# Four gate tiles by Strassen's scheme in the values' stage, and the first attention's queries and keys split on 128 partitions

## The chip, the cores and the metric

The kernel runs on one NeuronCore of a Trainium2 chip. The metric is the device time of one execution in microseconds. The core's engines run side by side, each through its own list of instructions in order: TensorE (PE in the profile, its weight loads PEld), VectorE (DVE), ScalarE (ACT), GpSimd (POOL) and SyncE (SP). DMA transfers are issued by SP, ACT and POOL, each into its own queue.

## The reference

One layer of a decoder trunk on 1024 positions and 1024 channels, all in float32.

```python
h = rms_norm(x, pre_mix_g)
proj = h @ w_in                     # 8192 columns
qa, ka, va, qb, kb, vb, gates = split(proj, ...)   # 512 512 512 1536 1536 1536 2048
# first attention: 4 heads, each two softmaxes of 64 dimensions, causal
qa, ka = rope(qa), rope(ka)
oa = (softmax(qa1 ka1) - lam * softmax(qa2 ka2)) @ va
ya = (rms_norm(oa) * 0.8) @ w_a_out
# second attention: 3 dilations x 4 heads of 128 dimensions, windows
yb = merge_of_dilations(qb, kb, vb) @ w_b_out
g_a, g_b = split(sigmoid(gates))
x = x + rms_norm((g_a * ya + g_b * yb) @ w_mix_out)
# gated MLP with a causal convolution of 3 taps
u = conv(rms_norm(x) @ w_up)
x = x + rms_norm((gelu(gate) * val) @ w_down)
```

(The factor 0.8 stands for 1 - lam_init, which is 0.8 lam_init being 0.2.)

## The kernel before

Every matrix product works on float32 operands split into two parts of a shorter format, a high one (ACT copies it, `split`, L149) and the rest (DVE subtracts, L146). `mm3` (L155 to L157) multiplies high by high, low by high and high by low: three matmuls for one product of 128 x 128 by 128 x 512.

The program runs in stages.

*The values' stage.* All values (va and vb, 2048 columns) are made in two sides of 1024 columns (`i` 0 and 1). Each side is a product of 2 x 2 blocks, done by Strassen's scheme in Winograd's form: seven products p1 to p7 for eight. Their left operands are blocks and sums of blocks of the transposed input: `b11`, `b21`, `b12`, `b22` lie in `xh`, `xl`, the sums in `t2`, `t3`, `t4`; a part of the first sum takes the place of `b12` until the product p6 of side 1, when `split_x` restores it. A list `steps_v` gives the order of the 56 steps (product, side, block of 128 rows); one step is 4 x 3 matmuls. `fetch_v` loads a step's weights on SP's queue, `ready_v` adds or subtracts weight blocks where a product needs it (`wz`) and splits them, five steps ahead, and `take_v` moves finished banks of PSUM into the quarters `yv`, which `put_v` sends to memory (`v_d`) on POOL's queue. The steps at which the first side's quarters are sent are in `STORE_AT`; other steps carry the norm, the angles, the sines and the tables of the rotation. Products on the right use the banks of the pools `ps_s` and `pt`, those on the left the pool `acc` and one bank of `ps_o`.

*The first attention.* A head's queries and keys come from `proj_t`, 2 halves x 8 blocks x 3 matmuls for each 128 columns. `rotated` applies the rotation with four copies of 32 partitions on ACT and three instructions on DVE. The two softmaxes of a head lie on partitions 0 to 63 (`u`) and 64 to 127 (`v`). `put_q` writes the high part of each into `a0`, `a1` and the low part into `b0`, `b1`, on 64 partitions each, and after the second half four transfers on POOL's queue (L754) copy them to the other 64 partitions. `put_k` writes the high part on one half of the partitions of `k0`, `k1` and the low part on the other. `attend_a` makes the scores of a block of 128 queries (L784, L785), takes minima and exponentials, joins the two softmaxes (L801), and every second block `turned` transposes them (L713) and `pv` multiplies by the values.

*The gates.* `gate(i)` is `proj_t` for one tile of 128 gate columns; `put_gate` scales it by the norm (DVE, L250) and sends it to memory on ACT's queue. The 16 gate tiles serve as filling work: `START_GATES` of them stand ahead of the first head, the letters g of `A_FILLS` are one gate each in the filling of heads 0 to 3 (p is the next head's projection, v and w the values of the second pair of heads, P, x, V belong to the second attention), and `B_GATES` of them run in the last step of the second attention. `interleave` spreads the filling over the steps of a head.

*Behind it* come the second attention, its merge of three dilations through memory, two output branches that read the gates back, the mixing product, and the MLP.

The order on each engine is written by a planner that simulates the program, with priorities from the code; `later` hangs work onto a count of steps.

Of the kernel before, what the change touches and what calls it, by code (L numbers as in the profile page):

```python
# [24 lines left out]
P = 128  # L25
# [21 lines left out]
NH = NF // 2  # L47
AHEAD, T1_AT, LAST = 4, 5, 7
MIX_UNITS = {3: (0,), 4: (1,), 5: (2, 4), 6: (5,), 7: (6, 3, 7)}
START_GATES, A_FILLS, B_GATES = 1, ("gpgg", "gpvgg", "wgpgg", "xgPVgg"), 3  # L50
SLOTS = 18
LEFT_PAD = 48


XT_BUFS, NORM_AT, ANGLES_AT, SINES_AT, TABLES_AT, STORE_AT = 6, 14, 25, 33, 34, {35: 0, 36: 3, 39: 2, 41: 1}

K_FIRST = (4, 0, 5, 1, 6, 2, 7, 3)
RSQRT_MAGIC = float(0x5F3759DF)
# [29 lines left out]
def trunk(ctx: ExitStack, tc: tile.TileContext, a, out):  # L88
# [252 lines left out]
    def f32(v):  # L341
        return v.bitcast(F32)
# [118 lines left out]
    with ExitStack() as st_y:  # L461
# [6 lines left out]
        def turns(pattern, *ps):  # L468

            ks = [iter(range(4)) for _ in ps]  # L470
            return [(ps[c], 1, next(ks[c])) for c in pattern]

        steps_v += [("p1", 1, k) for k in range(4)] + turns((0, 0, 1, 0, 1, 0, 1, 1), "p5", "p6")
        steps_v += turns((0, 0, 1, 1, 1, 1, 0, 0), "p3", "p7") + [("p4", 1, k) for k in range(4)]
        wz = [t[:, k % 2] for t in [wv.tile([P, 2, 512], F32, tag=f"wz{i}", name="wz") for i in range(2)] for k in range(2)]
        ready, got_v = {}, {}
# [10 lines left out]
        def new_y(name, pool=None):  # L487
            return [(pool or yv).tile([P, 512], F32, tag=f"y{name}{m}", name="yv") for m in range(4)]

        def fetch_v(n):  # L490
            p, i, k = steps_v[n]
            which = {"p1": ((0, 0),), "p2": ((0, 1),), "p5": ((1, 0), (1, 1)), "p6": ((0, 0),), "p7": ((0, 0), (1, 0)),
                     "p4": ((1, 1),), "p3": ((0, 1),)}[p]
            got_v[n] = [load_raw(a["w_v"][j * 4 + k][:, (2 * i + c) * 512 : (2 * i + c + 1) * 512], next(tags), parts=1 if n else 2)
                        for c, j in which]

        def ready_v(n, w=512):
            p, _, k = steps_v[n]
# [54 lines left out]
        quarter = {(0, i): new_y(f"a{i}") for i in range(2)}  # L553
        banks = {}

        def step_v(n):
            p, i, k = steps_v[n]
            x = xs_of[p]
            if p in ("p1", "p2", "p5") and k == 0:
                left = p == "p1"  # L560
                banks[left] = ([psum() for _ in range(3)] + [psum(F32, ps_o, "o")] if left else
                               [psum(F32, q, t) for q, t in ((ps_s, "s"), (pt, "pt")) for _ in range(2)])
            use = banks[p in ("p1", "p6", "p7", "p4")]
            wh, wl = ready.pop(n)
            for m in range(4):
                tk = slice(m * P, (m + 1) * P)
                mm3(use[m], x[0][:, k, tk], x[1][:, k, tk], wh, wl, k == 0 and p in ("p1", "p2", "p5"), k == 3, p in ("p6", "p7", "p4", "p3"))
            if k < 3:
                return
            with tc.high_priority(offset=80):  # L570
                for m in range(4):
                    take_v(p, i, m, use[m])
            if p == "p7" and i == 0:
                for m in range(4):
                    tt(quarter[3, 0][m], banks[False][m], quarter[3, 0][m], ALU.add)
# [56 lines left out]
        for n in range(8, len(steps_v)):  # L632
            p, i, k = steps_v[n]
            while fetched < min(n + (8 if n <= TABLES_AT else 10), len(steps_v)):
                fetch_v(fetched)
                fetched += 1
            while made < min(n + 5, len(steps_v)):
                ready_v(made)
                made += 1
            if 0 <= n - NORM_AT < 11:  # L640
                norm_x(n - NORM_AT)
            if n == NORM_AT + 11:
                lambda_scale()
            if n == TABLES_AT + 2:
                scale_tables(*args)
            if n == TABLES_AT + 4:
                tags = more_tags()
            if n == ANGLES_AT:
                pos = [load_raw(a["positions"][sl].partition_broadcast(P), next(tags)) for sl in halves()]
                args = [tb.tile([P, S], F32, tag=n_, name=n_) for n_ in ("sin", "cos")]  # L650
                angles(pos, *args, tb)
            if n in STORE_AT:
                put_v(STORE_AT[n], 0, True)
            if n == SINES_AT:
                make_sines(*args)
            if n == TABLES_AT:
                turn_norms()
            if k == 0 and (p, i) in places_y:
                q, name, pool = places_y[p, i]
                quarter[q, i] = new_y(name, pool)  # L660
            step_v(n)
            if k == 3 and i and p in ("p1", "p7", "p4", "p3"):
                put_v({"p1": 0, "p7": 3, "p4": 2, "p3": 1}[p], 1, p == "p1")
            if (p, i) == ("p5", 1):

                again.append(load_raw(a["xT"][k][:, 512:], next(tags)))
            if (p, i) == ("p6", 1):
                with behind_marks():
                    split_x(k, halves()[1], again[k])
# [15 lines left out]
                dma(v.rearrange("p (r ih) c -> p r ih c", ih=n)[:, :, ih], src[:, i * 4 // n : (i + 1) * 4 // n, ih])  # L685
        return vs

    def split_values(vs, res):

        with behind_marks():  # L690
            for v in vs:
                res.append(v_tiles())
                split(*res[-1], v)

    def rotated(ps, cos, sin, sl, quarter):
        t1 = rt.tile([P, 512], F32, tag="t1", name="t1")
        t2 = rt.tile([P, 512], F32, tag="t2", name="t2")
        for q in range(P // quarter):
            src, dst = slice((q ^ 1) * quarter, ((q ^ 1) + 1) * quarter), slice(q * quarter, (q + 1) * quarter)
            nc.scalar.activation(t1[dst], ps[src], AF.Copy)  # L700
        nc.vector.tensor_tensor(t2, ps, cos[:, sl], op=ALU.mult)  # L701
        nc.vector.tensor_tensor(t1, t1, sin[:, sl], op=ALU.mult)
        nc.vector.tensor_tensor(t2, t2, t1, op=ALU.add)
        return t2

    def v_tiles():
        return [slot(t, (P, 4, 256)) for t in ("vh", "vl")]
# [34 lines left out]
    def proj_a(h, res):  # L742
        a0, a1, b0, b1, k0, k1 = (slot(n) for n in ("a0", "a1", "b0", "b1", "k0", "k1"))
        res += [a0, a1, b0, b1, k0, k1]

        def put_q(half, sl, ps):
            t = rotated(ps, cos_a, sin_a, sl, 32)
            for part, hi in ((u, a0), (v, a1)):
                nc.scalar.activation(hi[part, sl], t[part], AF.Copy)
            for part, hi, lo in ((u, a0, b0), (v, a1, b1)):  # L750
                nc.vector.tensor_tensor(lo[part, sl], t[part], f32(hi[part, sl]), op=ALU.subtract)
            if half:
                for x, from_, to in ((a0, u, v), (a1, v, u), (b0, u, v), (b1, v, u)):
                    side(x[to], x[from_])  # L754

        def put_k(half, sl, ps):
            t = rotated(ps, cos_a, sin_a, sl, 32)
            for part, kk in ((u, k0), (v, k1)):
                nc.scalar.activation(kk[part, sl], t[part], AF.Copy)
            for part, to, kk in ((u, v, k0), (v, u, k1)):  # L760
                nc.vector.tensor_tensor(kk[to, sl], t[part], f32(kk[part, sl]), op=ALU.subtract)

        yield from proj_t(QA + h * P, put_q)
        yield from proj_t(KA + h * P, put_k)
# [104 lines left out]
        later(1, sums)  # L869
        later(3, norm)  # L870

    free_gates = list(range(2 * KC))

    def gates(n):

# [32 lines left out]
    def once(fn):  # L908

        fn()  # L910
        yield 0
# [13 lines left out]
    with st_a:  # L925
        ops = [[] for _ in range(AH)]
        vs = [[] for _ in range(AH // 2)]
        run(gates(START_GATES)[0])
        run(proj_a(0, ops[0]))
        split_values(fetch_values(1, 0), vs[0])  # L930
        of_pair = []
        for h in range(AH):
            out_sb, pair = {}, []
            todo = [functools.partial(attend_a, h, i, ops[h], vs[h // 2], out_sb, pair) for i in (6, 7, 4, 5, 2, 3, 0, 1)]
            kinds = {
                "p": lambda: (proj_a(h + 1, ops[h + 1]), 8),
                "v": lambda: (once(lambda: of_pair.extend(fetch_values(1, 256))), 0),
                "w": lambda: (once(lambda: split_values(of_pair, vs[1])), 0),
                "g": lambda: gates(1),
                "P": lambda: (proj_b(0, 0, ops_b[steps[0]]), 8),  # L940
                "x": lambda: (once(lambda: fetch_b(0, 0)), 0),
                "V": lambda: (once(lambda: split_b(0, 0)), 0),
            }
            if h + 1 == AH:
                tabs_b += load_tabs(0, 64)
            fills = [kinds[c]() for c in A_FILLS[h]]
            if h + 1 < AH:
                interleave(jobs(todo, a_weight), 52, *fills)
            else:
                interleave(itertools.chain(jobs(todo, a_weight), rest_due(12)), 64, *fills)  # L950
# [851 lines left out]
```

## Time and profile before

| what | value |
|---|---|
| median of three runs | 1685.25 us (1685.08 to 1686.24) |
| the profiled execution | 1684.85 us |
| its span | 1683.1 us |
| instructions | 22937 |
| data read from HBM, written to it | 177.54 MB, 47.86 MB |
| loads of weights from w_in | 96 of 256 KB |
| loads of weights for the values | 71 of 256 KB, 2 of 128 KB |
| stores of gates | 32 of 256 KB on ACT's queue |
| copies of a and b by POOL's queue | 16 of 256 KB |

The span runs from the first to the last instruction of the profiled execution; the device time has a little more around it. In rows of the timeline the first number is the start in us from the beginning of the span, the second the duration in us, and then engine, line, operation, out<-in, shape and count. In rows of groups the total in us and the mean in ns follow the count.

### The profile page before, as it was taken

The numbers are of one execution on the slowest core, as the hardware profiler recorded it, in microseconds if no ns is written. First come the engines' busy times: TensorE is split into PE (matmuls) and PEld (weight loads), VectorE is DVE, ScalarE is ACT, GpSimd is POOL, SyncE is SP. The second block draws the span as 40 slices with busy tenths as digits, with TensorE's granted clock in tenths as the row PEclk, the third lists the DMA queues.
The fourth block names the chain that finished last, engine by engine and source line by source line (L and its number), as shares of the span: only waits on it lengthen the run. The fifth ranks groups of instructions, "written<-read, shape, count | busy, mean of one in ns | idle before, by whom it ended". The sixth has DMA issues, their size and how long they took to land. (4 is left out here: it accounts for less than half of the span.)

```text
span 1683.1 us, 22937 instructions
## 1 busy us (share of the span) xinstructions
PE 1668.5 (99%) x7878; PEld 1394.0 (83%) x7878; DVE 1308.4 (78%) x2430; ACT 913.4 (54%) x1707; POOL 170.2 (10%) x267
## 2 busy tenths in 40 slices
PE   9999999999999999999999999999999999999997
PEld 7888888888888888888888888887888888888886
DVE  8795576877777777788766865988888778799978
ACT  7633574655445677667554533565554455255453
POOL 0031000000000000000123400022211121000000
PEclk9999999999999999999999999999999999999999
DMA  8767421315122212343676532267755655296524
GB/s 269 234 221 266 132 83 62 107 57 147 48 70 75 76 57 78 107 135 105 212 264 223 188 113 89 58 159 172 161 133 132 156 137 126 96 348 214 193 88 150
DMA packets 117253, 241.59 MB, mean 144 GB/s; under 512 B 14528, under 2 KB 23680, under 8 KB 117136
## 3 DMA queue, kind: packets, MB, share of 16 engines
q1 hardware_dynamic: 89296, 171.28, 30.6%
q0 software_dynamic: 23088, 60.45, 15.2%
q10 hardware_dynamic: 4752, 8.39, 1.3%
q8 instruction: 62, 1.02, 0.3%
q14 instruction: 55, 0.45, 0.1%
HBM read 177.54 MB, written 47.86 MB: 134 GB/s over the span
## 5 line engine op out<-in xcount | busy, mean ns | idle before, releaser
L157 PE MATMUL acc<-xl,whi 128*128 128x512 f32 x768 | 302.5, 394 | 0.0
L155 PE MATMUL acc<-xh,whi 128*128 128x512 f32 x768 | 302.0, 393 | 0.0
L156 PE MATMUL acc<-xh,wlo 128*128 128x512 f32 x768 | 301.7, 393 | 0.0
L149 ACT ACTIVATE whi<-raw 128x512 fp32r<-128x512 f32 (+1 forms) x249 | 154.1, 627 | 180.6 <-PE acc L157 115.4
L146 DVE TENSOR_TENSOR wlo<-raw,whi 128x512 fp32r<-128x512 f32 (+1 forms) x249 | 172.2, 700 | 32.8 <-ACT whi L149 27.9
L156 PEld LDWEIGHTS acc<-xh,wlo 128*128 128x128 f32 x768 | 144.4, 188 | 27.9
L157 PEld LDWEIGHTS acc<-xl,whi 128*128 128x128 f32 x768 | 144.4, 188 | 27.7
L155 PEld LDWEIGHTS acc<-xh,whi 128*128 128x128 f32 x768 | 144.5, 188 | 27.3
L155 PE MATMUL acc<-mh,whi 128*128 128x512 f32 x384 | 149.7, 390 | 1.7 <-ACT u L1447 1.3
L156 PE MATMUL acc<-mh,wlo 128*128 128x512 f32 x384 | 149.4, 389 | 0.0
L157 PE MATMUL acc<-ml,whi 128*128 128x512 f32 x384 | 149.1, 389 | 0.0
L700 ACT ACTIVATE t<-acc 64x512 f32<-64x512 f32 (+1 forms) x160 | 94.7, 592 | 62.0 <-PE acc L157 60.4
L149 ACT ACTIVATE whi<-s 128x512 fp32r<-128x512 f32 x80 | 49.8, 627 | 90.7 <-PE acc L157 63.5
L1443 DVE TENSOR_TENSOR u<-acc,u 128x512 f32<-128x512 f32 x100 | 68.5, 687 | 29.1 <-PE acc L157 28.9
L701 DVE TENSOR_TENSOR t<-acc,cos 128x512 f32<-128x512 f32 x64 | 44.2, 690 | 55.4 <-ACT t L700 51.9
L155 PEld LDWEIGHTS acc<-mh,whi 128*128 128x128 f32 x384 | 72.1, 188 | 17.7 <-ACT u L1447 2.2
L157 PEld LDWEIGHTS acc<-ml,whi 128*128 128x128 f32 x384 | 72.1, 188 | 14.9
L156 PEld LDWEIGHTS acc<-mh,wlo 128*128 128x128 f32 x384 | 72.1, 188 | 14.9
L1620 PE MATMUL acc<-whi,wlo 128*128 128x512 f32 x216 | 76.1, 390 | 0.0
L1619 PE MATMUL acc<-whi 128*128 128x512 f32 x216 | 74.8, 389 | 0.0
L1621 PE MATMUL acc<-wlo,whi 128*128 128x512 f32 x216 | 71.6, 390 | 0.0
L787 DVE CUSTOM_DVE_ANT_0 s<-s,mask_a 128x512 f32<-128x512 f32 (+3 forms) x96 | 52.5, 555 | 23.2 <-PE s L785 18.5
(402 smaller groups left out, 4015.2 us busy)
## 6 DMA issues: line engine op xcount, KB each, us to landing
raw<-in_w_in SPq DMA_DIRECT2D x96, 256.0 KB, 2.8
raw<-in_w_v SPq DMA_DIRECT2D x71, 256.0 KB, 4.6
raw<-in_w_up SPq DMA_DIRECT2D x68, 256.0 KB, 3.6
raw<-c_d SPq DMA_DIRECT2D x48, 256.0 KB, 3.6
c_d<-c SPq DMA_DIRECT2D x22, 512.0 KB, 4.0
s<-in_w_up POOLq DMA_DIRECT2D x40, 256.0 KB, 4.2
s<-s POOLq DMA_DIRECT2D x40, 256.0 KB, 3.9
raw<-in_w_down SPq DMA_DIRECT2D x37, 256.0 KB, 3.5
```

What stands on the lines that cost most here:

```text
L146: eng.tensor_tensor(lo, src, hi.bitcast(F32), op=ALU.subtract)
L149: copy = nc.scalar.activation(hi, src, AF.Copy)
L155: nc.tensor.matmul(o, sh, mh, start=first, stop=False, skip_group_check=on)
L156: nc.tensor.matmul(o, sl, mh, start=False, stop=False, skip_group_check=on)
L157: nc.tensor.matmul(o, sh, ml, start=False, stop=last, skip_group_check=on)
L700: nc.scalar.activation(t1[dst], ps[src], AF.Copy)
L701: nc.vector.tensor_tensor(t2, ps, cos[:, sl], op=ALU.mult)
L787: nc.vector.tensor_tensor_reduce(out=s_sb[:, c0:c1], in0=ps, in1=mask, scale=-scale, scalar=3.0e38, op0=ALU.add, op1=ALU.min, accum_out=mx ...
L1443: nc.vector.tensor_tensor(to, made(p), x, op=ALU.add)
L1619: nc.tensor.matmul(banks[m], gh[:, tk], wh, start=f == 0, stop=False)
L1620: nc.tensor.matmul(banks[m], gl[:, tk], wh, start=False, stop=False)
L1621: nc.tensor.matmul(banks[m], gh[:, tk], wl, start=False, stop=f == NH - 1)
```

## The change

Four of the 16 gate tiles, `gate_of(x, c)` = 12 to 15, are made in the values' stage as `PAIRS` = 2 pairs, by the same seven products; here the weights are the stationary operand and the input is the moving one. They stand behind the first side and p1 of the second, 14 steps of 4 x 3 matmuls, product by product with the two pairs in turn. Their results are added up in tiles that the quarters leave free, scaled (DVE) and sent on POOL's queue. One gate leaves the filling of each of heads 0, 1 and 2, and one leaves the last step of the second attention. `STORE_AT` moves the stores of the first side.

The rotation's result is split on all 128 partitions at once, into the tiles t1 and t2, and every piece of 64 partitions is placed by a transfer on POOL's queue: 8 for each half of the queries, 4 for each half of the keys. The values of the second pair of heads are split in halves.

```diff
-START_GATES, A_FILLS, B_GATES = 1, ("gpgg", "gpvgg", "wgpgg", "xgPVgg"), 3
+PAIRS, START_GATES, A_FILLS, B_GATES = 2, 1, ("gpg", "gpvg", "wgpg", "xgPVgg"), 2
-..., STORE_AT = ..., {35: 0, 36: 3, 39: 2, 41: 1}
+..., STORE_AT = ..., {32: 0, 37: 3, 42: 2, 46: 1}
...
-        steps_v += [("p1", 1, k) for k in range(4)] + turns((0, 0, 1, 0, 1, 0, 1, 1), "p5", "p6")
+        steps_v += [("p1", 1, k) for k in range(4)]
+        steps_v += [(p, "gate", x) for p in ("p2", "p1", "p5", "p6", "p7", "p4", "p3") for x in range(PAIRS)]
+        steps_v += turns((0, 0, 1, 0, 1, 0, 1, 1), "p5", "p6")
...
+        def gate_of(x, c):
+            return 2 * (KC - PAIRS + x) + c
...
+            if i == "gate":
+                srcs = [w_in[where[GT + gate_of(k, c) * P]][:, j * 512 : (j + 1) * 512] for c, j in which]
+            else:
+                srcs = [a["w_v"][j * 4 + k][:, (2 * i + c) * 512 : (2 * i + c + 1) * 512] for c, j in which]
+            got_v[n] = [load_raw(src, next(tags), parts=1 if n else 2) for src in srcs]
...
+        def take_gate(p, n, use):
+
+            def put(q):
+                sl = halves()[q % 2]
+                y = gate_y[n][q]
+                tt(y, use if p == "p4" else y, rstd_row[:, sl], ALU.mult)
+                nc.gpsimd.dma_start(gt_d[gate_of(n, q // 2)][:, sl], y)
+
+            y = gate_y[n]
+            if p in ("p2", "p6", "p7"):
+                nc.scalar.activation(y[{"p2": 0, "p6": 1, "p7": 3}[p]], use, AF.Copy)
+            if p == "p1":
+                tt(y[0], use, y[0], ALU.add)
+                put(0)
+            if p == "p7":
+                tt(y[3], banks[n, False], y[3], ALU.add)
+                put(3)
+            if p == "p4":
+                put(2)
+            if p == "p3":
+                tt(y[1], use, y[1], ALU.add)
+                put(1)
+
+        def step_gate(p, n, wh, wl):
+
+            left = p in ("p1", "p6", "p7", "p4")
+            if p in ("p1", "p2"):
+                banks[n, left] = psum(F32, pt, "pt") if left else psum(F32, ps_s, "s")
+            x, use = xs_of[p], banks[n, left]
+            for k in range(4):
+                c = slice(k * P, (k + 1) * P)
+                mm3(use, wh[:, c], wl[:, c], x[0][:, k], x[1][:, k], k == 0 and p in ("p1", "p2", "p5"), k == 3, ...)
+            with tc.high_priority(offset=80):
+                take_gate(p, n, use)
...
+            if (p, i, k) == ("p2", "gate", 0):
+                ya, yb = new_y("a0"), new_y("b3", yw)
+                gate_y.update({x: {0: ya[x], 1: ya[2 + x], 3: yb[x], 2: yb[2 + x]} for x in range(PAIRS)})
...
-    def split_values(vs, res):
+    def split_values(vs, res, parts=4):
...
-                split(*res[-1], v)
+                for b in range(0, 4, parts):
+                    split(*(t[:, b : b + parts] for t in (*res[-1], v)))
...
+        def split_rotated(t):
+            t, other = t
+            hi, lo = other.bitcast(F32R), t.bitcast(F32R)
+            nc.scalar.activation(hi, t, AF.Copy)
+            nc.vector.tensor_tensor(lo, t, other, op=ALU.subtract)
+            return hi, lo
+
         def put_q(half, sl, ps):
-            t = rotated(ps, cos_a, sin_a, sl, 32)
-            for part, hi in ((u, a0), (v, a1)):
-                nc.scalar.activation(hi[part, sl], t[part], AF.Copy)
-            for part, hi, lo in ((u, a0, b0), (v, a1, b1)):
-                nc.vector.tensor_tensor(lo[part, sl], t[part], f32(hi[part, sl]), op=ALU.subtract)
-            if half:
-                for x, from_, to in ((a0, u, v), (a1, v, u), (b0, u, v), (b1, v, u)):
-                    side(x[to], x[from_])
+            t = rotated(ps, cos_a, sin_a, sl, 32, True)
+            hi, lo = split_rotated(t)
+            for x, src, part in ((a0, hi, u), (a1, hi, v), (b0, lo, u), (b1, lo, v)):
+                for to in (u, v):
+                    side(x[to, sl], src[part])
 
         def put_k(half, sl, ps):
-            t = rotated(ps, cos_a, sin_a, sl, 32)
-            for part, kk in ((u, k0), (v, k1)):
-                nc.scalar.activation(kk[part, sl], t[part], AF.Copy)
-            for part, to, kk in ((u, v, k0), (v, u, k1)):
-                nc.vector.tensor_tensor(kk[to, sl], t[part], f32(kk[part, sl]), op=ALU.subtract)
+            t = rotated(ps, cos_a, sin_a, sl, 32, True)
+            hi, lo = split_rotated(t)
+            for x, src, part, to in ((k0, hi, u, u), (k0, lo, u, v), (k1, hi, v, v), (k1, lo, v, u)):
+                side(x[to, sl], src[part])
...
-    free_gates = list(range(2 * KC))
+    free_gates = list(range(2 * (KC - PAIRS)))
...
-                "w": lambda: (once(lambda: split_values(of_pair, vs[1])), 0),
+                "w": lambda: (once(lambda: split_values(of_pair, vs[1], 2)), 0),
```

More of the change, by code (lines that the diff above doesn't have):

```diff
@@ L49 @@
 MIX_UNITS = {3: (0,), 4: (1,), 5: (2, 4), 6: (5,), 7: (6, 3, 7)}
-START_GATES, A_FILLS, B_GATES = 1, ("gpgg", "gpvgg", "wgpgg", "xgPVgg"), 3
+PAIRS, START_GATES, A_FILLS, B_GATES = 2, 1, ("gpg", "gpvg", "wgpg", "xgPVgg"), 2
 SLOTS = 18
 LEFT_PAD = 48
-XT_BUFS, NORM_AT, ANGLES_AT, SINES_AT, TABLES_AT, STORE_AT = 6, 14, 25, 33, 34, {35: 0, 36: 3, 39: 2, 41: 1}
+XT_BUFS, NORM_AT, ANGLES_AT, SINES_AT, TABLES_AT, STORE_AT = 6, 14, 25, 33, 34, {32: 0, 37: 3, 42: 2, 46: 1}
 K_FIRST = (4, 0, 5, 1, 6, 2, 7, 3)
@@ L493, in fetch_v @@
                      "p4": ((1, 1),), "p3": ((0, 1),)}[p]
-            got_v[n] = [load_raw(a["w_v"][j * 4 + k][:, (2 * i + c) * 512 : (2 * i + c + 1) * 512], next(tags), parts=1 if n else 2)
-                        for c, j in which]
+            if i == "gate":
[3 more added lines that the diff above has]
+            got_v[n] = [load_raw(src, next(tags), parts=1 if n else 2) for src in srcs]
         def ready_v(n, w=512):
@@ L554, in trunk @@
         banks = {}
+        gate_y = {}
+        def take_gate(p, n, use):
[25 more added lines that the diff above has]
+                c = slice(k * P, (k + 1) * P)
+                mm3(use, wh[:, c], wl[:, c], x[0][:, k], x[1][:, k], k == 0 and p in ("p1", "p2", "p5"), k == 3, p in ("p6", "p7", "p4", "p3"))
+            with tc.high_priority(offset=80):
+                take_gate(p, n, use)
         def step_v(n):
             p, i, k = steps_v[n]
+            if i == "gate":
+                step_gate(p, k, *ready.pop(n))
+                return
             x = xs_of[p]
@@ L692, in split_values, with rotated @@
                 res.append(v_tiles())
-                split(*res[-1], v)
-    def rotated(ps, cos, sin, sl, quarter):
+                for b in range(0, 4, parts):
+                    split(*(t[:, b : b + parts] for t in (*res[-1], v)))
+    def rotated(ps, cos, sin, sl, quarter, both=False):
         t1 = rt.tile([P, 512], F32, tag="t1", name="t1")
@@ L703, in rotated @@
         nc.vector.tensor_tensor(t2, t2, t1, op=ALU.add)
-        return t2
+        return (t2, t1) if both else t2
     def v_tiles():
```

## The prediction

> **What bounds the kernel now.** I read the first part of the page (busy time), then the waits of TensorE, then the matmuls in order of time, and last the busy time of every engine stage by stage.
>
> ```profile
> span 1683.1 us, 22937 instructions
> PE 1668.5 (99%) x7878; PEld 1394.0 (83%) x7878; DVE 1308.4 (78%) x2430; ACT 913.4 (54%) x1707; POOL 170.2 (10%) x267
> ```
>
> The waits of TensorE (who, for whom: us in total, times, longest):
>
> ```profile
> PE acc L155 <- ACT xh L387: 1.4, 1, 1.4
> PE acc L155 <- DVE ya L1211: 1.4, 2, 0.9
> PE acc L155 <- ACT u L1447: 1.3, 1, 1.3
> PE pt L594 <- DVE t4l L591: 1.2, 1, 1.2
> PE acc L155 <- ACT mh L149: 0.3, 1, 0.3
> PE acc L156 <- DVE xl L383: 0.2, 1, 0.2
> ```
>
> The reader is to see that the six waits add up to 5.8 us of 1683. TensorE is fed from end to end, so the time is the sum of its instructions, and a matmul taken away is worth what it occupies, until something starves. What it occupies is not the duration that the page gives. The group of the projections' and gates' matmuls, and three rows from the first projection (start, us, what), then the last row of that unbroken run:
>
> ```profile
> L157 PE MATMUL acc<-xl,whi 128*128 128x512 f32 x768 | 302.5, 394 | 0.0
> ...
> 178.07 0.39 PE L155 MATMUL acc<-xh,whi 128*128 128x512 f32 x1
> 178.30 0.39 PE L156 MATMUL acc<-xh,wlo 128*128 128x512 f32 x1
> 178.53 0.39 PE L157 MATMUL acc<-xl,whi 128*128 128x512 f32 x1
> ...
> 203.46 0.39 PE L156 MATMUL acc<-xh,wlo 128*128 128x512 f32 x1
> ```
>
> Each lasts 0.39 us, but the next one starts 0.23 us later: they overlap. From 178.07 to 203.46 there are 113 matmuls, hence 25.39 / 112 = 0.2267 us each. That is the price I use.
>
> The stages (us; busy time and instructions of PE, PEld, DVE, ACT, POOL; clock, DMA share, GB/s). The values' stage ends at 161.8; then the first gate and head 0's projections; heads 0, 1, 2 of the first attention, each from its first score to the next head's; the end of the second attention, where the last gates are; the first output branch:
>
> ```profile
> 100.00:161.80 61.80, 61.80 (x279) 51.23 (x278) 47.63 (x84) 25.08 (x41) 21.48 (x33) 1.00 0.76 262
> 161.80:203.70 41.90, 41.90 (x187) 34.70 (x186) 19.14 (x29) 20.71 (x34) 4.44 (x9) 1.00 0.54 162
> 203.70:275.50 71.80, 71.80 (x351) 60.31 (x350) 53.96 (x128) 43.48 (x90) 2.06 (x4) 1.00 0.25 78
> 275.50:350.10 74.60, 74.60 (x380) 63.11 (x379) 56.88 (x154) 41.50 (x89) 2.06 (x4) 1.00 0.28 89
> 350.10:426.10 76.00, 76.00 (x387) 64.27 (x386) 59.28 (x156) 44.17 (x92) 2.07 (x4) 1.00 0.38 104
> 815.00:852.50 37.50, 37.50 (x194) 31.86 (x193) 24.07 (x62) 23.63 (x48) 6.44 (x11) 1.00 0.74 252
> 852.50:905.00 52.50, 51.14 (x230) 41.77 (x229) 34.47 (x59) 15.84 (x25) 12.98 (x23) 1.00 0.70 232
> ```
>
> TensorE is busy in all of every stage but the last, where its 1.4 us wait for DVE lies.
>
> **The gates' matmuls.** A gate is 2 halves x 8 blocks x 3 = 48 matmuls, four are 192. By the scheme a pair is 7 products x 4 blocks x 3 = 84, two pairs 168. All are 128x512. So 24 go: 24 x 0.2267 = **5.44 us less**. The values' stage grows by 168 x 0.2267 = 38.1 us; each of heads 0, 1, 2 and the last step of the second attention shrinks by 48 x 0.2267 = 10.88 us.
>
> **What the values' stage takes on.** Rows for its new work, all in DVE's groups of the first 500 us and in the page's DMA issues:
>
> ```profile
> L146 DVE TENSOR_TENSOR wlo<-wz,whi 128x512 fp32r<-128x512 f32 x24 | 16.2, 689 | 0.1
> L345 DVE TENSOR_TENSOR wz<-raw,wz 128x512 f32<-128x512 f32 x8 | 5.5, 692 | 9.6 <-DMA raw<-in_w_v 9.6
> L250 DVE TENSOR_TENSOR gate<-acc,rstd_row 128x512 f32<-128x512 f32 x26 | 17.9, 688 | 10.4 <-PE acc L157 10.4
> raw<-in_w_in SPq DMA_DIRECT2D x96, 256.0 KB, 2.8
> v_d<-yv POOLq DMA_DIRECT2D x32, 256.0 KB, 5.2
> ```
>
> DVE: 14 splits, 8 sums of weights (p5, p6, p7, p3 of each pair) and 14 sums and scalings of results, 36 x 0.69 = 24.8 us in 38.1. The late part of the stage had 47.63 of 61.8 (77%) and gets 72.4 of 99.9 (72%). The 18 weight loads on SP's queue (1, 1, 2, 1, 2, 1, 1 a pair, against 8 before) and 8 stores now on POOL's queue are 6.8 MB in 38.1 us, 179 GB/s, below the 262 of that part. The values' stores that move to later steps leave more room. Operands are made five steps (5 x 12 x 0.2267 = 13.6 us) ahead. So I take 0. One seam is tight: the values' p5 takes over the banks that the gates' last p3 leaves, and DVE reads the last of these (0.69 us) while three matmuls (0.68 us) run. Bounds 0 and one step, 2.7 us; I take 0.3, since TensorE can begin on the other two banks.
>
> **What the heads lose.** A gate takes 2 splits and 2 scalings of DVE with it, 4 x 0.69 = 2.8 us. The new rotation takes one DVE and one ACT instruction from each of four half projections a head: two on 64 partitions become one on 128, and the former cost as much as one on 128:
>
> ```profile
> L761 DVE TENSOR_TENSOR k<-t,k 64x512 fp32r<-64x512 f32 x16 | 11.0, 687 | 0.5
> L749 ACT ACTIVATE a<-t x16: 615/630/633, 183.3 to 381.3; 64x512 fp32r<-64x512 f32 x16
> ```
>
> That is another 2.8 us of DVE and 2.5 of ACT. DVE in heads 0 to 2: (53.96 - 5.6) / 60.9 = 79%, 80%, 82%, from 75, 76 and 78. No engine becomes the bound. The chain can still be too slow: DVE makes the probabilities (L801), TensorE turns them (L713). The closest in-order pair I found is in head 1:
>
> ```profile
> 326.89 1.02 DVE L801 SCALAR_TENSOR_TENSOR s<-s,ratio 128x768 f32<-128x768 f32 x1
> 329.51 0.27 PE L713 MATMUL pt<-ident,s 128*128 128x128 f32 x1
> ```
>
> It has 329.51 - 327.91 = 1.6 us to spare; a pair of query blocks gets 10.88 / 4 = 2.7 us shorter. If the chain kept its pace it would lose 1.1 us here. The two rotations save it 1.3 us of DVE and ACT each. Bounds 0 and 3.3 (once a head); I take 0.2. The values of the second pair of heads are split in halves: 4 x 0.69 instead of 2 x 1.22 us of DVE, 0.3 us, off the path.
>
> **The placing by transfers.** Per head 24 transfers of 64 partitions replace 4:
>
> ```profile
> L754 POOL DMA_DIRECT2D a<-a x8 | 4.2, 521 | 209.0 <-ACT a L749 208.1 <-issue 0.7
> b<-b POOLq DMA_DIRECT2D x8, 256.0 KB, 4.7
> 203.69 0.39 PE L784 MATMUL s<-k,a 128*128 128x512 f32 x1
> 205.29 1.40 DVE L761 TENSOR_TENSOR k<-t,k 64x512 fp32r<-64x512 f32 x2
> 208.45 0.33 PE L784 MATMUL s<-k,a 128*128 128x384 f32 x1
> ```
>
> POOL: 24 x 0.52 = 12.5 us a head, under 2.1 before, of 61; what queues behind a waiting transfer there is only the next transfer of this head. The keys were written in place, the second half at 206.69, and a score read it at 208.45. Now 4 issues (2.1 us) and a landing (4.7) follow, less 1.3 us of ACT and DVE: 5.5 us later. In head 0 the scores wait for it; what covers it is the first gate and the first fill gate, 2 x 10.88 us that need nothing of head 0. In heads 1 to 3 a whole gate still stands between the projection and the next head. The tiles t1 and t2 are held till the landing, two evacuations of 5.44 us apart: 10.9 us against 2.4 (four copies) + 1.3 + 4.2 (8 issues) + 4.7 = 12.6 for the queries; that delays an evacuation by 1.7 us, and three accumulators cover it. Bounds 0 and 5.5, I take 0.2.
>
> **The last step.** It drops from 37.5 to 26.6 us. DVE needs 24.07 - 2.8 = 21.3 of it (80%), ACT 23.63 - 1.3 = 22.4 (84%). This is the tightest place. The merge's transfers run beside it, and the wait for DVE in the branch behind it may go (-1.4) or grow. Bounds -1.4 and the whole gate, 10.9; I take 0.
>
> **Sum.** -5.44 + 0.3 + 0.2 + 0.2 = -4.7 us. The profiled execution took 1684.85 us (1.75 around the span), 0.4 below the median of the three runs, 1685.25. So 1684.85 - 4.7 = 1680.1 for such an execution, 1680.5 for the median.
>
> By the Trainium skill ("TensorE: Matmul & The Clock Gate", Back-to-back issue gap) a stream of weight load and matmul pairs sustains about 131 ns at 512 columns; the 24 would then be an estimated 3.1 us and the sum 1682.8. The same section's gap of a single matmul, 512 / 2.4 + 2.5 = 216 ns, gives an estimate of 5.2. The trace has 0.2267 us over 113, so the first does not hold here and the second nearly does.
>
> **Rivals.** (1) *The last step is bound by its chain, not by TensorE.* For it: ACT at 84% there, work in order on ACT and DVE, merges through memory. Against it: between two of its score blocks TensorE ran nothing but gates for 8 us,
>
> ```profile
> 828.26 0.27 PE L157 MATMUL s<-kl,qh 128*128 128x128 f32 x1
> 836.61 0.22 PE L155 MATMUL s<-kh,qh 128*128 128x128 f32 x1
> ```
>
> which shows room for a closer spacing, and ACT falls to 30% (15.84 of 52.5) right behind. Price up to 10.88, so 1680.5 + 10.9 = 1691.4; slower from 8.1 us of it on (-4.7 + 8.1 = 3.4), no change from 1.4 on. (2) *Head 0's keys come late.* For it: +5.5 us on keys that were read 1.8 us after they were written. Against it: the fill. Fully bare 1680.5 + 5.3 = 1685.8, no change. The Trainium skill ("SBUF — State Buffer", SBUF: two separate sides) says that POOL's transfers can't get their descriptors while DVE runs a two-port perf-mode instruction, which speaks for later keys still; the trace shows POOL's issue at 521 ns in heads where DVE is busy 75% of the time, so no such hold is seen. (3) *A matmul is worth its duration*, 24 x 0.394 = 9.5 us: 1676.5. The rows of starts are against it.
>
> **How the numbers follow.** A measurement of this kernel can tell about 0.2%, 3.4 us. Forecast 0.66 (1679 to 1682); part of a gate lost in the last step or head 0's keys late 0.19 (1682 to 1688); the last step's gate lost whole 0.10 (to 1691); more gained than the sum says, rival 3 or an old wait gone, 0.05. The range 1678 to 1688 leaves out the last two. Faster: 0.66 + 0.05; same: most of the 0.19; slower: the rest.
>
> **What would show it.** 7854 matmuls for 7878; L155 to L157 with acc<-xh or xl at 704 each; the gap between starts still 0.2267; heads 0 to 2 each about 10.9 us shorter; the values' stage 38 us longer with no new wait; the four groups of transfers 96 times with about 0.5 us of POOL each. Wrong would be a wait of TensorE over 2 us on a placed tile, on L787, L801 or a bank's reader in the values' stage, or idle time around the last step.

## The result, and the profile after

The changed kernel took 1709.88 us (median of four runs, 1707.29 to 1711.29) against 1685.16 (1684.88 to 1686.24) of the kernel before on the same chip: 24.7 us more, a ratio of 1.0146 with an interval of 1.0130 to 1.0161. The forecast was 1680.5 in a range of 1678 to 1688. The profiled execution took 1707.29 us.

The first part of the page of the changed kernel (span, then busy time, share and instructions of each engine):

```profile
span 1705.2 us, 23101 instructions
PE 1674.9 (98%) x7854; PEld 1394.6 (82%) x7854; DVE 1312.0 (77%) x2436; ACT 908.5 (53%) x1705; POOL 213.5 (13%) x355
```

The 24 matmuls are gone (7854 for 7878), and yet TensorE is busy 6.4 us longer, 1674.9 for 1668.5, and idle 30.3 us of its span (1705.2 - 1674.9) for 14.6. The span is 22.1 us longer: 15.7 of it more idle time, 6.4 more busy time. By cadence the busy time should have fallen by 5.4, so 11.8 us of it are not work that was added. Most of this is matmuls at half clock: the three stretches of the last section hold 16.7 us of busy time, which at full clock would be some 8 (an estimate). The rest was not taken apart.

The waits of TensorE in the changed kernel (who, for whom: us in total, times, longest):

```profile
PE acc L155 <- ACT obh L149: 4.0, 2, 3.7
PE s L839 <- DVE mx L842: 2.8, 3, 2.3
PE acc L155 <- DVE t L753: 2.0, 2, 1.0
PE acc L155 <- ACT xh L387: 2.0, 2, 1.4
PE acc L155 <- DVE gl L1298: 1.6, 1, 1.6
PE s L157 <- DVE kl L951: 1.4, 1, 1.4
PE pt L765 <- ACT rows L1106: 1.3, 1, 1.3
...
PE pt L155 <- ACT yv L576: 1.2, 1, 1.2
```

Before, six waits made 5.8 us. The new ones belong to the scores of the first attention (L839 was L784, L842 was L787), the rotation (L753), the second attention (L951, L1106) and the output branches (`obh`, L1298). Only one of the new ones, the last row, lies in the values' stage; it comes at 130.4 us, between two products of the gates.

The busy time by stage in the changed kernel (us; busy time and instructions of PE, PEld, DVE, ACT, POOL; clock, DMA share, GB/s): the values' stage; from there to head 0's first score; heads 0, 1 and 2, each from its first score to the next head's; then three short stretches picked out because TensorE runs dry in them:

```profile
100.00:200.20 100.20, 99.02 (x441) 81.71 (x440) 70.22 (x119) 34.44 (x59) 22.75 (x39) 1.00 0.67 234
200.20:250.30 50.10, 49.11 (x217) 40.40 (x216) 20.51 (x30) 21.32 (x34) 15.40 (x30) 1.00 0.68 180
250.30:326.00 75.70, 75.70 (x368) 63.52 (x367) 51.41 (x127) 47.25 (x97) 20.13 (x40) 1.00 0.47 125
326.00:395.30 69.30, 69.30 (x356) 58.71 (x355) 52.05 (x147) 36.78 (x82) 7.79 (x16) 1.00 0.37 99
395.30:458.50 63.20, 58.59 (x291) 48.79 (x290) 49.34 (x144) 34.35 (x80) 9.18 (x18) 0.95 0.46 124
405.00:416.00 11.00, 7.44 (x31) 5.41 (x30) 10.63 (x30) 9.86 (x21) 0.00 (x0) 0.82 0.34 115
578.00:600.00 22.00, 18.54 (x118) 16.18 (x117) 17.35 (x51) 16.74 (x47) 0.00 (x0) 0.92 0.19 59
912.00:940.00 28.00, 22.31 (x82) 16.74 (x81) 16.92 (x23) 7.97 (x13) 7.90 (x13) 0.84 0.66 225
```

The values' stage is as forecast: 100.2 us for 61.8, that is 38.4 more, with 1.2 idle. The heads are not. Before they took 71.8, 74.6 and 76.0 us, 222.4 together; now 75.7, 69.3 and 63.2, 208.2. They give back 14.2 us and not 3 x 10.88 = 32.6, and 8.2 of that go into the time between the values' stage and head 0's first score (50.1 us for 41.9). Head 0 even grew, with 368 matmuls for 351: the planner put work there that stood later. Head 2, with only 291 matmuls, runs dry. What is missing there is missing again at the start of the second attention (578 to 600) and at the second output branch (912 to 940). I call these places the third head, the second attention and branch b. By cadence: take from the time between two matmuls' starts what a matmul of so many columns takes where TensorE is fed, and add up the excess over the whole trace. It is 27.7 us more than before; less 5.4 this is the 22 us of the span, and about 26 us of it lie in these three places (9, 8 and 9).

What the engines do at the third head, DVE first, then TensorE (start, us, what; in brackets the idle time before it and its releaser):

```profile
408.63 1.15 DVE L856 SCALAR_TENSOR_TENSOR s<-s,ratio 128x896 f32<-128x896 f32 x1
409.70 1.28 DVE L146 TENSOR_TENSOR vl<-vperm,vh 128x512 fp32r<-128x512 f32 x2
...
410.97 0.41 DVE L881 TENSOR_TENSOR osb<-osb,o 128x256 f32<-128x256 f32 x1
411.30 0.68 DVE L146 TENSOR_TENSOR vl<-vperm,vh 128x512 fp32r<-128x512 f32 x1
411.90 0.68 DVE L842 CUSTOM_DVE_ANT_0 s<-s,mask_a 128x512 f32<-128x512 f32 x1
...
418.77 0.69 DVE L753 TENSOR_TENSOR t<-acc,cos 128x512 f32<-128x512 f32 x1
```

```profile
412.65 0.79 PE L839 MATMUL s<-k,a 128*128 128x512 f32 x1 [2.31 <-DVE mx L842]
...
419.61 0.47 PE L155 MATMUL acc<-xh,whi 128*128 128x512 f32 x1 [1.04 <-DVE t L753]
```

DVE is busy 10.63 of 11.00 us. It joins the softmaxes, splits the values and only then reads the score bank that TensorE waits for (L842 at 411.90); the next projection, behind the scores in TensorE's order, waits for DVE too, for the rotation to read an accumulator (L753 at 418.77).

The groups that answer to the rest of the forecast, TensorE's and POOL's of the changed kernel:

```profile
L155 PE MATMUL acc<-xh,whi 128*128 128x512 f32 x704 | 277.6, 394 | 2.0 <-DVE t L753 2.0
L157 PE MATMUL acc<-xl,whi 128*128 128x512 f32 x704 | 277.4, 394 | 0.0
```

```profile
L810 POOL DMA_DIRECT2D b<-t x32 | 16.6, 532 | 3.6 <-PE s L840 2.3 <-DMA b<-t 0.5 <-DVE rc L854 0.3
L810 POOL DMA_DIRECT2D a<-t x32 | 16.6, 529 | 116.7 <-ACT t L801 64.2 <-ACT osb L880 51.0 <-PE s L840 1.2
L816 POOL DMA_DIRECT2D k<-t x32 | 16.5, 522 | 59.0 <-ACT t L801 56.5 <-DVE t L802 1.3 <-DVE mx L842 0.5
```

### The profile page after: what moved, and what is told of

Its sections match the earlier page's. It is cut to its first block, busy times and chain, and to the rows that moved or that the text cites. A ratio compares the mean times of both kernels' runs of the same rounds, so it can differ in the third digit from the quotient of the medians.

```text
span 1705.2 us, 23101 instructions
## 1 busy us (share of the span) xinstructions
PE 1674.9 (98%) x7854; PEld 1394.6 (82%) x7854; DVE 1312.0 (77%) x2436; ACT 908.5 (53%) x1705; POOL 213.5 (13%) x355
## 5 line engine op out<-in xcount | busy, mean ns | idle before, releaser
L155 PE MATMUL acc<-xh,whi 128*128 128x512 f32 x704 | 277.6, 394 | 2.0 <-DVE t L753 2.0
L156 PE MATMUL acc<-xh,wlo 128*128 128x512 f32 x704 | 277.6, 394 | 0.0
L157 PE MATMUL acc<-xl,whi 128*128 128x512 f32 x704 | 277.4, 394 | 0.0
L155 PEld LDWEIGHTS acc<-xh,whi 128*128 128x128 f32 x704 | 132.8, 189 | 28.2 <-ACT whi L149 1.4
L156 PEld LDWEIGHTS acc<-xh,wlo 128*128 128x128 f32 x704 | 132.7, 188 | 25.6
L157 PEld LDWEIGHTS acc<-xl,whi 128*128 128x128 f32 x704 | 132.7, 188 | 25.3
L753 DVE TENSOR_TENSOR t<-acc,cos 128x512 f32<-128x512 f32 x64 | 44.1, 690 | 54.7 <-ACT t L752 51.4
L156 PEld LDWEIGHTS acc<-mh,wlo 128*128 128x128 f32 x384 | 72.1, 188 | 14.8
L842 DVE CUSTOM_DVE_ANT_0 s<-s,mask_a 128x512 f32<-128x512 f32 (+3 forms) x96 | 52.3, 553 | 22.1 <-PE s L840 17.1
```

The costliest lines, as they stand in the source:

```text
L155: nc.tensor.matmul(o, sh, mh, start=first, stop=False, skip_group_check=on)
L156: nc.tensor.matmul(o, sl, mh, start=False, stop=False, skip_group_check=on)
L157: nc.tensor.matmul(o, sh, ml, start=False, stop=last, skip_group_check=on)
L842: nc.vector.tensor_tensor_reduce(out=s_sb[:, c0:c1], in0=ps, in1=mask, scale=-scale, scalar=3.0e38, op0=ALU.add, op1=ALU.min, accum_out=mx ...
```

## The experiments

Two theories to begin with. F: the gates that were taken away were what TensorE did beside chains that are bound elsewhere; those chains keep their length, so the time of the gates comes back as idle time. P: the placing by transfers makes operands late. Each group of runs has its own chip, and the kernel before was run again on it; so across groups the differences to the kernel before are compared.

**The two halves alone, and two other spreads of the gates.** `e1_gates` is the changed kernel with the old `put_q` and `put_k`; `e2_place` the kernel before with the new ones; `e3_fill12` and `e4_last3` only move gates:

```diff
 e3_fill12 (from the changed kernel)
-START_GATES, A_FILLS, B_GATES = 1, ("gpg", "gpvg", "wgpg", "xgPVgg"), 2
+START_GATES, A_FILLS, B_GATES = 0, ("gpg", "gpvgg", "wgpgg", "xgPVg"), 2
 e4_last3 (from the changed kernel)
+START_GATES, A_FILLS, B_GATES = 1, ("gpg", "gpvg", "wgpg", "xgPVg"), 3
```

> The gates' half of the change alone: two pairs by the seven products in the values' stage and one gate less in heads 0, 1, 2 and in the last step, but the queries and keys split and placed as before. Theory F (fill): without those gates the first attention's own chain (scores, minima, exponentials, turning) sets the pace, TensorE draws later projections forward and runs dry; then this is still slow, 1696 to 1708 us, with idle stretches and a drop of the granted clock. Theory P (placing): the transfers hold t1 and t2 and block the next projection; then this one is at 1679 to 1682 us.

> The other half alone: queries and keys split on 128 partitions and placed by transfers, the values of the second pair of heads in halves, all 16 gates where they were. Theory F: the fill is whole, so TensorE stays busy, 1683 to 1688 us. Theory P: 1694 us or more, with a wait at the head whose queries land late.

> The whole change, but the twelve gates that are left are spread anew: none ahead of head 0, and the heads 2, 3, 3 and 2 gates (instead of one ahead and 2, 2, 2, 3). Theory F: the dry stretch at the start of head 2 (near 404 to 419 us) goes and the time falls by 6 to 10 us, to 1700 to 1704. Theory P: the stretch stays, as the queries of head 3 still wait for their slots: 1707 to 1712.

> The whole change, but the last step of the second attention has its three gates again and head 3 two instead of three. If the idle 9 us in the output branches (928 to 941 us) come from the gate that left the last step, they go: about 1701 us, if head 3 does without its gate. If they come from work that is late for another reason, they stay, and the time is 1708 or more.

The kernel before took 1684.85 here. `e1_gates` took 1704.48 (ratio 1.0118, 1.0103 to 1.0133), 19.6 more, with the same three dry places. `e2_place` took 1689.58 (1.0024, 1.0014 to 1.0034), 4.7 more, with one new wait, in head 0. That lies between what F and P had said for it. The two add up to 24.3 of the 24.7: the placing is good for a fifth of the loss, the gates for the rest. `e3_fill12` took 1703.41 (1.0109, 1.0094 to 1.0124): at the third head TensorE was idle 2.6 us for 4.6 and its clock stayed whole, but a wait of 3.9 us (4.1 by cadence) appeared in head 0; the other two places stayed. `e4_last3` took 1707.00 (1.0122, 1.0100 to 1.0143), between its two forecasts and not clear of the changed kernel: the idle stretch at branch b was gone, and a wait of 3.2 us appeared at 542 us, behind the head that had given its gate, with one of 2.5 us in head 0, where no gate had been moved. A gate that is moved moves the gap.

**What one gate is worth at each place.** Gates were left out of the kernel before, with nothing added to the values' stage (these kernels don't compute the reference's result; they put a price on a piece of work):

```diff
-START_GATES, A_FILLS, B_GATES = 1, ("gpgg", "gpvgg", "wgpgg", "xgPVgg"), 3
+START_GATES, A_FILLS, B_GATES = 1, ("gpgg", "gpvg", "wgpgg", "xgPVgg"), 3   # m1_head1
+START_GATES, A_FILLS, B_GATES = 0, ("gpgg", "gpvgg", "wgpgg", "xgPVgg"), 3  # m2_start
+START_GATES, A_FILLS, B_GATES = 1, ("gpgg", "gpvgg", "wgpgg", "xgPVgg"), 2  # m3_last
+START_GATES, A_FILLS, B_GATES = 1, ("gpg", "gpvg", "wgpg", "xgPVgg"), 2     # m4_four
```

> The kernel before with one gate of head 1's fill left out altogether: gate 15 is not computed (its readers take gate 14). 48 matmuls less, 10.9 us by column cadence. Theory F (the chain of the first attention's heads sets their pace, the gates are what TensorE does beside it): the heads together shrink by less than half a gate, the projections are drawn forward in its place, and an idle stretch appears where they run out, at the end of the heads or at the start of the second attention: 1677 to 1682 us. Rival R (the heads had room for a gate each; the loss comes from what the values' stage takes on or from where the removed gates stood elsewhere): 1674 us and no new idle stretch over 2 us.

> The kernel before with the gate ahead of head 0's projections left out altogether (gate 15 is not computed, its readers take gate 14). It stands before the first chain begins. Theory F: nothing of the heads' chain is beside it, so it is worth all or nearly all of its 10.9 us: 1674 to 1677 us, with the heads as long as before. Rival: it covers the wait for the rotation's tables or head 0's keys: some 5 us of idle time before the first score or projections drawn into that place, 1679 to 1682.

> The kernel before with one of the three gates of the second attention's last step left out altogether (gate 15 is not computed, its readers take gate 14). Theory F, which sees the gate there as cover of the last step's chain and of the merge behind it: TensorE waits 5 to 9 us for the merged heads of output branch b, 1679 to 1684 us. Rival R (the last step has room): 1674 us, no wait over 2 us at the output branches.

> The kernel before with four gates left out altogether, from the places where the change takes them (heads 0, 1, 2 and the last step); gates 12 to 15 are not computed, their readers take gate 11. 192 matmuls less, 43.5 us by cadence. Theory F: it shows the same three idle stretches as the changed kernel (third head, start of the second attention, second output branch; 20 to 25 us together) and saves only about half: 1661 to 1667 us. Rival R (the loss of the changed kernel comes from what was added to the values' stage): 1641 to 1645 us with TensorE as full as before.

Against 1684.75 of the kernel before: the gate at the start saved 10.0 us (1674.72; 0.9941, 0.9929 to 0.9953), the gate of head 1 4.5 (1680.24; 0.9972, 0.9961 to 0.9983), the gate of the last step 1.7, which is not clear of nothing (1683.05; 0.9991, 0.9981 to 1.0002), and the four of the change together 19.5 (1665.25; 0.9884, 0.9871 to 0.9898), each of 10.9, or of 43.5 for the four. All four times came out as F had them (TensorE's waits at branch b in `m3_last`, 3.2 and 1.6 us, are just under the 5 to 9 forecast), and `m4_four` shuts out that the loss comes from what the values' stage took on: with nothing added there the same three places run dry. The change adds 38.1 + 0.3 us there and gets 19.5 back, 18.9 more; `e1_gates` measured 19.6.

Where the gate of head 1 went, in two windows of `m1_head1` (head 3 up to its last score, then the start of the second attention):

```profile
428.30:502.90 74.60, 74.60 (x380) 63.11 (x379) 55.38 (x149) 36.02 (x76) 0.00 (x0) 1.00 0.17 57
560.00:582.00 22.00, 20.11 (x101) 17.45 (x102) 19.91 (x44) 18.00 (x40) 0.00 (x0) 0.84 0.26 85
```

Nothing is idle in the heads, nor are they shorter: by the first scores, head 1 is 74.9 us long for 74.6. Projections were drawn forward in the gate's place, and the lack shows some 200 us behind the edit, where they should have been.

And the last step's, in `m3_last`: the wait of TensorE, then POOL's issue of the merge's broadcasts and the sum that needs them:

```profile
PE acc L155 <- ACT obh L149: 3.2, 2, 2.8
```

```profile
894.32 1.62 POOL L1094 DMA_DIRECT2D mw<-e_d  x3 [1.60 <-DVE om L1110]
...
902.93 1.76 DVE L1107 TENSOR_TENSOR mw<-og,mw 128x1536 f32<-128x1536 f32 x1 [7.21 <-DMA mw<-e_d]
```

The second half of the merge reuses the tile `mw` of the first; it is issued when DVE has done with that, DVE waits 7.21 us for it, and branch b's operands follow. The last of them is ready at 907.5 us, for 909.0 in the kernel before: with 10.9 us of TensorE's work gone in front of it, this chain ends 1.4 us earlier.

**What binds the chains, and the two other waits.** `d1_dve` and `d2_act` both lighten the heads of `m4_four`, the one for DVE, the other for ACT (condensed; these two leave out part of the result as well):

```diff
 d1_dve
-scalar_tensor_tensor(sc[0][:, :w], sc[1][:, :w], ratio, sc[0][:, :w], ...)
+scalar_tensor_tensor(sc[0][:, :P], sc[1][:, :P], ratio, sc[0][:, :P], ...)
-split(vh, vl, v); res.append((vh, vl))
+activation(vh, v, AF.Copy); res.append((vh, vh))
 d2_act
-exp = activation(sc[c][:, :w], sc[c][:, :w], AF.Exp, ...)
+exp = activation(sc[c][:, :P], sc[c][:, :P], AF.Exp, ...)
 m5_merge (from m3_last)
-mw, og: [P, BG, 512], bufs=1
+mw, og: [P, BG, 256], bufs=2      # load(0), load(1), add(0), load(2), ...
 e5_values (from e2_place)
-run(proj_a(0, ops[0])); split_values(fetch_values(1, 0), vs[0])
+early_v = fetch_values(1, 0); run(proj_a(0, ops[0])); split_values(early_v, vs[0])
```

> m4_four (four gates left out) with less work for DVE in the first attention's heads and the same for the others: the difference of the two probabilities is formed for the first 128 columns only, and the low half of the values is left out (the high one is used twice); 24 us of DVE in 290. Theory D (what is left when the gates go is DVE, which works in order and is 99% busy in the idle stretch at 365 to 376 us, TensorE's scores and the projections' accumulators waiting for it): the stretch at the third head falls under 4 us, the one at the second attention's start gets smaller, 1650 to 1658 us. Rival L (the latency of the whole chain scores, exponentials, turns sets the pace): 1660 to 1665, as it shortens only a little. The stretch at output branch b stays for both.

> m4_four with less work for ACT in the first attention's heads and the same for DVE: the exponentials are taken of the first 128 columns only (both maps; the mask's fill is -1 to keep the rest finite); some 26 us of ACT in 290, and the chain from score to turn is shorter by it. Theory D (DVE): no gain, 1662 to 1666 us, the stretch at the third head still 8 us or more. Rival L (latency of the chain): at least the gain of d1_dve, 1650 to 1658.

> m3_last (one gate of the last step left out altogether) with the merge of the second attention's heads worked in four quarters of 256 columns through two buffers each of half the size, so that the next quarter's transfers don't wait for the sums of the one before. Theory M (the 9 us at output branch b are the reload of the merge's single buffers: DVE waits 7 us there for the weights' broadcasts): the stretch falls under 4 us, 1675 to 1678 us. Rival: the last step's chain itself is late: 1681 to 1684 us as in m3_last.

> e2_place (the placing alone) with the first values' transfers issued ahead of head 0's projections and not behind them. Theory Q (the 2.8 us wait in head 0 comes from ACT, which stands 5.8 us behind the copy of values that haven't landed, with the keys' second evacuation queued behind it): the wait at 205 us goes, 1685 to 1687.5 us. Rival: the tiles held until the placing lands are what delays the evacuation: the wait stays, 1688 to 1691.

The kernel before took 1685.06 here. `d1_dve` took 1657.02 (0.9835, 0.9822 to 0.9849), 28.0 less, for 19.5 in `m4_four`; `d2_act` took 1664.36 (0.9883, 0.9870 to 0.9897), 20.7 less, no clear gain. The third head in `m4_four`, then in `d2_act`, and the heads as a whole in `m4_four` and in `d1_dve`:

```profile
365.00:376.00 11.00, 5.79 (x24) 4.18 (x24) 10.88 (x25) 4.86 (x8) 2.07 (x4) 0.78 0.41 95
...
200.00:500.00 300.00, 294.79 (x1466) 247.85 (x1465) 225.75 (x588) 170.98 (x357) 6.31 (x12) 0.98 0.25 78
```

```profile
365.00:376.00 11.00, 6.91 (x18) 4.31 (x19) 10.88 (x24) 4.95 (x11) 2.07 (x4) 0.67 0.47 119
```

```profile
200.00:500.00 300.00, 299.60 (x1516) 253.15 (x1515) 214.78 (x605) 173.96 (x367) 6.20 (x12) 1.00 0.27 82
```

With ACT lighter DVE still shows 10.88 of 11.00 us and TensorE 6.91; with DVE lighter TensorE is busy 299.6 of 300. So DVE's work binds the third head, by a queue that is local: over the 300 us DVE is at 75%. A full DVE alone is not enough, though. The kernel before has such stretches in heads 0, 1 and 2, and TensorE loses nothing in them:

```profile
228.00:239.00 11.00, 11.00 (x55) 9.23 (x54) 10.79 (x24) 8.92 (x17) 2.06 (x4) 1.00 0.55 144
305.80:316.80 11.00, 11.00 (x63) 9.49 (x63) 10.80 (x32) 9.16 (x18) 0.00 (x0) 1.00 0.55 184
361.40:372.40 11.00, 11.00 (x53) 9.09 (x52) 10.77 (x22) 7.35 (x13) 0.00 (x0) 1.00 0.13 46
```

There TensorE runs 53 to 63 matmuls while DVE is full; at the third head of `m4_four` it runs 24 and is dry between them. The place at the second attention stayed in both, against the forecast that it would get smaller: TensorE is idle 4.7 us there in `d1_dve` (528 to 552 us) as in `m4_four` (538 to 562). What binds it was not tested.

`m5_merge` missed: 1685.29 (1.0002, 0.9993 to 1.0011), 0.2 more than the kernel before, where `m3_last` took 1.7 less. The smaller pieces made more transfers on POOL's one queue, DVE still stood 5.8 and 4.9 us before two of the four pieces, and waits for `ya` and `oah` of branch a came on top. That the merge's transfers end last at branch b is read from the trace; that more buffers would help isn't shown.

`e5_values` took 1685.48 (1.0006, 0.9997 to 1.0014), 0.4 more than the kernel before: 4.3 of the placing's 4.7 us are gone. In `e2_place` the wait came about like this, ACT's rows first, then DVE's and TensorE's:

```profile
201.36 1.06 ACT L149 ACTIVATE vh<-vperm 128x1024 fp32r<-128x1024 f32 x1 [5.80 <-DMA vperm<-v_d]
202.45 2.39 ACT L701 ACTIVATE t<-acc 32x512 f32<-32x512 f32 x4
```

```profile
207.25 0.69 DVE L702 TENSOR_TENSOR t<-acc,cos 128x512 f32<-128x512 f32 x1
```

```profile
208.09 0.47 PE L155 MATMUL acc<-xh,whi 128*128 128x512 f32 x1 [2.84 <-DVE t L702]
```

The evacuation of the keys' second half was queued on ACT behind a copy of values that were still on their way from memory, and DVE's part of it came some 10 us later (207.25; in the kernel before, where the line is L701, 197.09). With the values fetched earlier ACT starts it at 197.65 for 202.45, and TensorE has no wait there.

**Half of the change.** One pair of gates instead of two (`PAIRS` 1), so that only two gates are taken away; and the whole change with the values fetched early:

```diff
+PAIRS, START_GATES, A_FILLS, B_GATES = 1, 0, ("gpgg", "gpvgg", "wgpgg", "xgPVgg"), 2  # c3_pair, old placing
+PAIRS, START_GATES, A_FILLS, B_GATES = 1, 0, ("gpgg", "gpvg", "wgpgg", "xgPVgg"), 3   # c4_pair, early_v
+PAIRS, START_GATES, A_FILLS, B_GATES = 2, 0, ("gpg", "gpvgg", "wgpgg", "xgPVg"), 2    # c5_early, early_v
```

> Half of the change: one pair of gates (14 and 15) by the scheme in the values' stage, the old placing, and the two gates taken from where they cost most to miss and least: the one ahead of head 0's projections and one of the last step. If the prices of single gates add up: 84 x 0.2267 = 19.0 + 0.3 us more in the values' stage, 10.1 saved at the start (m2_start), 1.7 in the last step (m3_last): 1685.1 + 7.5 = 1692.6 us (1691 to 1695), one idle stretch of 7 to 10 us at output branch b. Rival (the prices don't add, the places share one shortage or the values' stage costs more than its matmuls): outside that.

> Half of the change with the placing by transfers, the first values' transfers issued early as in e5_values, and the two gates taken ahead of head 0 and from head 1. If prices add: 1685.1 + 0.4 (e5_values) + 19.3 - 10.1 - 4.5 = 1690.2 us. Theory D adds that the placing's lighter rotation (2.8 us of DVE a head less) gives the heads room, so the gate of head 1 is worth up to its whole 10.9: down to 1684. So 1684 to 1690; without that effect 1690 to 1692. A version that beats both kernels would need 1681 or less, which neither gives.

> e3_fill12 (the whole change, no gate ahead of head 0, twelve gates spread 2, 3, 3, 2 and 2) with the first values' transfers issued early. Theory Q: its 4.1 us wait in head 0 at 233 us is ACT behind values that haven't landed, as in the placing alone: 1698 to 1700 us, the wait gone, the stretches at 580 and 920 us unchanged. Rival: the shortage only moves on: 1702 to 1704, with another stretch longer by the same.

Against 1685.56: `c3_pair` 1698.54 (1.0077, 1.0058 to 1.0096) and `c4_pair` 1699.84 (1.0085, 1.0070 to 1.0099), both slower than expected, by 6 and 10 us; `c5_early` 1699.25 (1.0080, 1.0063 to 1.0096), as theory Q had it, 13.7 more than the kernel before for 18.6 in `e3_fill12`. The first two have a cost that the whole change hasn't: the values' stage takes longer than its matmuls, which the rival of `c3_pair` had named. Late in the values' stage, `c3_pair` and then the changed kernel:

```profile
105.00:135.00 30.00, 24.34 (x106) 18.43 (x105) 24.71 (x46) 7.89 (x14) 13.02 (x22) 1.00 0.99 361
```

```profile
110.00:140.00 30.00, 28.82 (x127) 23.54 (x126) 26.40 (x45) 9.55 (x17) 8.97 (x16) 1.00 1.03 380
```

The DMA engines are full in both; with one pair TensorE loses 5.7 of 30 us for 1.2. (A product is a single step then, and the next one's operands have half the time; that this is the reason was only argued.) And in `c4_pair` the third head ran dry again (TensorE idle 3.6 of the 14 us from 390 on, the clock 0.79), so the rotation's 2.8 us of DVE a head did not make its gate free. No version that computes everything beat the kernel before: of the prices measured only the gate at the start is worth nearly all of its matmuls, there is one of it, and the matmuls of a pair cost 19.0 us.

## Why the prediction was wrong, point by point

- *What a matmul is worth* (0.2267 us, 24 of them 5.44): right. Where TensorE is fed and its clock is whole the gap is 0.23, and the counts came as said: 7854, 704 in each group.
- *What the values' stage takes on* (0, and 0.3 for the seam): right. 38.4 us more; the one wait, 1.2 us, is not at the seam that I had named but between the gates' own products, where ACT still reads a bank.
- *What the heads lose* (bounds 0 and 3.3, taken 0.2) is the step that failed. I took the heads to shrink by the whole of each gate because no engine was full on the average (79 to 82% for DVE), and bounded the chain's part by the one spare time of 1.6 us that I had found. The three gates gave back 17.8 of 32.6 us (19.5 for four, less 1.7 for the last step's), so the term was 14.8. This is far outside the bounds. Two things were missed. DVE is at its limit for 11 us at a stretch, where the value splits, the rotation and the reduction of the scores come together; the kernel before has such stretches too (10.8 of 11 us), and a mean over the head hides them. And the planner moves projections forward into any place that a gate leaves, so that the heads look full and the lack comes out at the first place that has none left. For the third head `d1_dve` and `d2_act` show that DVE binds; for the second attention, where about half of the term comes out, the cause stays open.
- *The last step* (bounds -1.4 and 10.9, taken 0): rival 1 in its size, 9.2 of 10.9, though the 1.7 behind this is uncertain by about as much. Of the reasons that rival 1 gave, work in order on ACT and DVE and merges through memory, the trace has the wait at the last: the second load of the merge. That its single buffer is the reason isn't shown, as `m5_merge` missed. The wait that I had quoted there, TensorE's for `ya`, belongs to branch a; in the kernel before DVE already waits 8.5 us in all for the merge's broadcasts (852 to 930 us, the longest 5.1), which I had not looked at.
- *The placing* (bounds 0 and 5.5, taken 0.2): 4.7 us, 4.3 of them from something not in the step, the values' copies ahead of the evacuation on ACT. POOL's part was right: 96 transfers at 522 to 532 ns. Head 0's first score came 8.8 us later in `e2_place` for the 5.5 said; all but 2.8 us of it were covered, and TensorE's work used there is missing later.
- The sum with these sizes: -5.4 + 0.3 + 14.8 + 9.2 + 4.7 = 23.6 us, against 24.7 measured. No term stood for the clock; the some 8 us of matmuls at half clock are part of the 14.8 and the 9.2.
- *What would make it wrong* named a wait of over 2 us on L787; it came (L842 now, 2.3 us).

## What to carry to other kernels

That TensorE is busy 99% does not make every matmul worth its time: filling work is worth it only until the chain beside it is bare, and a scheduler that pulls later work forward hides the lack until far behind the edit. Before taking fill away, look for the stretches in which an in-order engine beside it is full over ten microseconds, not for its share of the stage: they show where fill may be needed, not that it will be. Then leave out one piece at each place, with nothing added, to see its price. Of the three places tried singly here one paid 10.0, one 4.5 and one 1.7 of 10.9 us.

## What the runs showed of the hardware

The granted clock fell to half inside the run at each dry place of the changed kernel, and it never did so before ahead of the end of the run. Two windows around the third head, and matmuls of branch b in such a stretch and behind it:

```profile
405.00:412.00 7.00, 4.08 (x18) 2.28 (x16) 6.93 (x20) 5.91 (x12) 0.00 (x0) 1.00 0.10 39
412.00:418.80 6.80, 5.91 (x22) 5.20 (x22) 6.29 (x27) 6.68 (x16) 0.00 (x0) 0.50 0.48 158
```

```profile
933.13 0.63 PE L155 MATMUL acc<-obh,whi 128*128 128x512 f32 x1
933.56 0.63 PE L156 MATMUL acc<-obh,wlo 128*128 128x512 f32 x1
...
941.52 0.39 PE L155 MATMUL acc<-obh,whi 128*128 128x512 f32 x1
941.75 0.39 PE L156 MATMUL acc<-obh,wlo 128*128 128x512 f32 x1
```

At half clock a matmul starts every 0.43 us for 0.23. The three stretches lasted 6.8, 3.4 and 10.2 us, with 5.9, 3.4 and 7.4 us of busy time in them; half of that, some 8 us, is an estimate of what the clock cost, on top of 15.7 us more idle time. Not every dry place pays it: in `c3_pair` TensorE waited 2.9 and 2.3 us at branch b and the clock stayed whole. The Trainium skill ("TensorE: Matmul & The Clock Gate", Part 1: The HAM clock gate) tells of a free-running window of 3413 ns, at half rate after an idle one; one, two and three of these windows are what the trace shows. Its advice to avoid gaps of more than about 3 us (the same page, Why this matters for your kernels) is not enough here: the clock fell at 412.0 after 7 us in which TensorE was busy 4.08, with no wait over 2.31, and at the second attention (596.3) with no wait over 1.4. In the 3.4 us before these two falls TensorE was busy 0.85 and 2.0 us.
